# A hybrid decoder step on one core: state pieces loaded one step ahead, their update pinned on ScalarE

## The chip, the cores and the metric

One Trainium2 chip, one NeuronCore (core 0). The metric is the device time of one execution in microseconds; lower is better. The engines are called by the profile's names: PE (TensorE matmuls), PEld (TensorE weight loads), DVE (VectorE), ACT (ScalarE), POOL (GpSimd), SP (SyncE, which issues the weight DMAs here).

## The reference

One inference step of a one-layer decoder for 272 prompt tokens (16 meta tokens and 256 new ones) and 8 sample tokens, each of a running sequence:

```python
u = rmsnorm(h, pre_mix_g)
mix, conv_buf, ssm_h, ret_s = mixers(u, ...)   # SSD heads and retention heads
h = h + rmsnorm(mix @ w_out, post_mix_g)
f = rmsnorm(h, pre_ffn_g)
f = (silu(f @ w_gate) * (f @ w_up)) @ w_down
h = h + rmsnorm(f, post_ffn_g)
```

For the sample tokens the mixers also return the new states, and these concern us here. Each is an old state times a decay plus an outer product with the new token: `hg = exp(last) * hg + (wts * x) B^T` for the 16 SSD heads, `s = exp(c * lg) * s + k v^T` for the 4 retention heads. The SSD states of the 8 sequences are 4 MB, the retention states 8 MB; each has to be read and written back once for the update. They feed nothing else in the step.

## The kernel before

All weights (some 210 MB in fp32) stream through the core in pieces of 128 x 1024, 512 KB each. `Stream.block` (L113) brings one piece in eight blocks: SP loads it into `raw` (4 buffers, L122), ACT copies it into `hi` in a rounded matmul format (3 buffers, L123), and DVE takes the rest `raw - hi` into `lo` (3 buffers, L124). `three` (L130) multiplies each 128 x 128 block with the activations, which are split the same way, in three matmuls: `hi` with the high part (L132), `hi` with the low part (L133), `lo` with the high part (L134). A piece thus serves 24 matmuls, and `gemm` (L136) sums up 16 blocks (2 pieces) in PSUM before its result is evicted.

The stages run in order: the input projection with the mixers between its matmuls, `w_out` (tiles `o`), the two feed-forward matrices (tiles `f`, gate and up blocks in turn, 88 results), and `w_down` (tiles `d`). The change lies in the feed-forward stage. There `ev_f` (L842) evicts each result: for an even one DVE scales it (L846) and ACT takes its silu (L848); for an odd one DVE scales it, multiplies the two (L851), ACT rounds the product into `ah` (L852) and DVE takes the rest into `al` (L853). Up to `m` = 39 of the 44 pairs, 24 of these odd evictions carry a state step. Such a step first copies one column on POOL (`pace`, L857), which waits for L851 and so ties the step to that moment; then it calls `ret_state` (L816, 16 pieces, tile `su`) or `ssm_state` (L825, 8 pieces, tile `hu`), two of the first to one of the second.

One state piece is 128 x 1024, 512 KB: POOL loads it (L819, L828), ACT multiplies it by its decay in place (L820, L829), DVE adds the outer product in 4 instructions of 256 columns (L822) or 8 of 128 columns (L831), and POOL stores it (L86). The pieces live in the pool `sd` with 3 buffers under one tag.

The order on each engine is made when the kernel is built, by a planner that simulates the program and issues what is ready, by priority, which is the place in the program. The `hi` and `lo` of a weight piece are raised by 1500 places. `keep_in_program_order` fixes an instruction behind the last one that was traced on the same engine before it; `pinned` (L219) does so for a POOL DMA. Here `pace` and the load are fixed in this way, while the ACT copy of a state piece stands wherever the planner saw its data ready. At run time each engine takes its instructions strictly in that order.

Of the kernel before, what the change touches and what calls it, by code (L numbers as in the profile page):

```python
# [9 lines left out]
AF = mybir.ActivationFunctionType  # L10
# [5 lines left out]
P = 128  # L16
# [37 lines left out]
def hybrid_step(ctx: ExitStack, tc: tile.TileContext, wall, xT, pp, cc, dmask, cs, convst, ssm, ret,  # L54
                yT, oconv, opssm, opret, osssm, osret):
    nc = tc.nc
    V, A, G, T = nc.vector, nc.scalar, nc.gpsimd, nc.tensor
    MULT, ADD, SUB, MAX, MIN = ALU.mult, ALU.add, ALU.subtract, ALU.max, ALU.min
# [12 lines left out]
    def slot(name, w=NA, n=4, dt=F32):  # L71
        return sp.tile([P, n, w], dt, name=name, tag="s")

    def small(name, w=NA):
        t = ta.tile([P, 308], F32, name=name, tag="t")
        return t[:, :w]

    def bank(name, w=512):
        t = pm.tile([P, 512], F32, name=name, tag="m")
        return t[:, :w]  # L80

    def table(name):
        return tc.keep_in_program_order(A.preload_act_table_set(name))

    def load(out, in_):
        G.dma_start(out, in_)  # L86
# [9 lines left out]
    def con(n, i=0, w=None):  # L96
        w = CC[n][1] - i if w is None else w
        return ccs[:, CC[n][0] + i:CC[n][0] + i + w]
# [55 lines left out]
                three(ps[:, :n], xh, xl, k == 0, k == nk - 1)  # L154
            evict(m, ps[:, :n])

    # u = x * g, split in two parts
    table("sqrt_and_others")
    xs = [slot(f"x{i}") for i in range(4)]
    uh = [slot(f"uh{i}", dt=F32R) for i in range(4)]  # L160
# [29 lines left out]
        i, j = divmod(k, 4)  # L190
        return uh[i][:, j, NA - n:NA], ul[i][:, j, NA - n:NA]

    # token norms
    sxn = cp.tile([P, 64], F32, name="sxn")
    sbn = cp.tile([P, P], F32, name="sbn")
    skn = cp.tile([P, 64], F32, name="skn")
    svn = cp.tile([P, 256], F32, name="svn")
# [8 lines left out]
    def token_norms():  # L206
        pr = bank("pr", NA)
        for i in range(2):
            T.matmul(pr, ones, xsum[:, i, :], start=(i == 0), stop=(i == 1))
        with tc.high_priority(offset=1500):  # L210
            A.activation(rbc, pr, AF.Sqrt, bias=eps, scale=1.0 / DM)
            V.reciprocal(rbc, rbc)

        # rotary tables with the token norm
        for i in range(2):
            V.tensor_tensor(tabs[:, i, :], css[:, i, :], rbc, MULT)
            A.mul(tabs[:, 2 + i, :], tabs[:, i, :], 1.0 / 16.0)

    def pinned(out, in_):  # L219
        tc.keep_in_program_order(G.dma_start(out, in_))  # L220
# [7 lines left out]
            pinned(cst, convst)  # L228
            pinned(dms, dmask)

# [1 line left out]
    bc = slot("bc")  # L232
    xc = [slot(f"xc{i}") for i in range(2)]
    cst = tp.tile([P, 12, NB, 3], F32, name="cst")
# [2 lines left out]
    dasel = cp.tile([P, 1], F32, name="dasel")  # L237
# [90 lines left out]
    def ev_first(m, ps):  # L328
        if m == 0:
            token_norms()  # L330
            held["dt"] = do_dt(ps)
            next(held["dt"])
        else:
            do_xbc(m - 1, ps)
# [6 lines left out]
            next(held["dt"])  # L341
    load(oconv, cout.rearrange("p a b c -> p a (b c)"))

# [1 line left out]
    def nat_lhs(name, src):  # L345
        m = tp.tile([P, NB, 8, 2], F32, name=name, tag="nl", bufs=2)
        for half in range(2):
            for i in range(2):
                V.tensor_scalar(m[:, :, 4 * i:4 * i + 4, half].rearrange("p b t -> p t b"), src[i], con("pm", half, 1),
                                None, MULT)  # L350
        return m.rearrange("p b t h -> p (b t h)")
# [6 lines left out]
    COLS = ((0, 256, 0), (256, 400, 112), (400, 416, 240))  # L358
    MCOLS = ((0, 256, 16), (256, 400, 0), (400, 416, 104))

# [1 line left out]
    y1 = [slot(f"y1_{i}", NO) for i in range(2)]  # L362
    y2 = [slot(f"y2_{i}", NO) for i in range(2)]
    btok = slot("btok", 256, 3)
# [117 lines left out]
                                   ps[:, hp * 8:hp * 8 + 8], MULT, ADD)  # L482
        yield

# [1 line left out]
    kf = [slot(f"kf{i}") for i in range(2)]  # L486
    qf = [slot(f"qf{i}", NO) for i in range(2)]
    vsm = [tp.tile([P, 4, NB], F32, name=f"vsm{i}", tag=f"vsm{i}", bufs=1) for i in range(2)]
# [139 lines left out]
                A.copy(o, ps)  # L628
                load(opret[:, m, :], o)

# [1 line left out]
    def rstds(name, groups, scale, outs=None, load_table=True):  # L632
        pss = []
        for g, sums in enumerate(groups):
            ps = bank(f"{name}{g}", NO)
            for i, s in enumerate(sums):
                T.matmul(ps, ones, s, start=(i == 0), stop=(i == len(sums) - 1))
            pss.append(ps)
        if load_table:
            table("natural_log_exp_and_others")  # L640
        rs = outs or [small(f"{name}r{g}", NO) for g in range(len(groups))]
        sc = scale if isinstance(scale, list) else [scale] * len(groups)
        with tc.high_priority(offset=1000):
            for ps, r, c in zip(pss, rs, sc):
                A.activation(r, ps, AF.Ln, bias=eps, scale=c)
            for r in rs:
                A.activation(r, r, AF.Exp, scale=-0.5)
        return rs
# [97 lines left out]
    for g in (ssd, kt, ssmp, scr, rsm, rsm2, yr, rsq, nrm, n10):  # L746
        assert next(g, None) is None

# [1 line left out]
    def min_(k, n):  # L750
        i, j = divmod(k, 4)
        return mh[i][:, j, :], ml[i][:, j, :]
# [29 lines left out]
    for k in range(KT):  # L782
# [12 lines left out]
        elif k < KT - 1:  # L795
            n = small(f"hs{k}", NO)
# [9 lines left out]
    def ffn_norm():  # L806
        rstds("n4", [[ha, hb]], 1.0 / DM, [rhc], False)

# [1 line left out]
    mix.close()  # L810
    ex = ctx.enter_context(tc.tile_pool(name="ex", bufs=NEXTRA))
    def fin(k, n):
        i, j = divmod(k, 4)
        return fh[i][:, j, :], fl[i][:, j, :]

    def ret_state(c):  # L816
        sb = sd.tile([P, 4, 256], F32, name=f"su{c}", tag="st")
        tc.keep_in_program_order(
            G.dma_start(sb, ret[:, c * 1024:(c + 1) * 1024].rearrange("p (a v) -> p a v", v=256)))  # L819
        A.activation(sb, sb, AF.Copy, scale=con("gam"))  # L820
        for a in range(4):
            V.scalar_tensor_tensor(sb[:, a, :], svn, skn[:, 4 * c + a:4 * c + a + 1], sb[:, a, :], MULT, ADD)  # L822
        load(osret[:, c * 1024:(c + 1) * 1024].rearrange("p (a v) -> p a v", v=256), sb)

    def ssm_state(c):  # L825
        sb = sd.tile([P, 8, P], F32, name=f"hu{c}", tag="st")
        tc.keep_in_program_order(
            G.dma_start(sb, ssm[:, c * 1024:(c + 1) * 1024].rearrange("p (a n) -> p a n", n=P)))  # L828
        A.activation(sb, sb, AF.Copy, scale=dasel)  # L829
        for a in range(8):  # L830
            V.scalar_tensor_tensor(sb[:, a, :], sbn, sxn[:, 8 * c + a:8 * c + a + 1], sb[:, a, :], MULT, ADD)  # L831
        load(osssm[:, c * 1024:(c + 1) * 1024].rearrange("p (a n) -> p a n", n=P), sb)

    def aslot(name, i):
        if i < FT // 4 - NEXTRA // 2:
# [6 lines left out]
    def ev_f(m2, ps):  # L842
        m, up = divmod(m2, 2)
        i, j = divmod(m, 4)
        t = small(f"f{m2}", NO)
        V.tensor_tensor(t, ps, rhc, MULT)  # L846
        if not up:
            A.activation(t, t, AF.Silu)  # L848
            held[m] = t
            return  # L850
        V.tensor_tensor(t, t, held.pop(m), MULT)  # L851
        A.copy(ah[i][:, j, :], t)  # L852
        V.tensor_tensor(al[i][:, j, :], t, ah[i][:, j, :].bitcast(F32), SUB)  # L853
        n = m * 24 // 40
        if m < 40 and (m + 1) * 24 // 40 > n:
            pace = ta.tile([P, 1], F32, name=f"pace{m}", tag="pace", bufs=2)
            tc.keep_in_program_order(G.tensor_copy(pace, t[:, 0:1]))  # L857
            if n % 3 == 2:
                ssm_state(n // 3)
            else:  # L860
                ret_state(n // 3 * 2 + n % 3)

    gemm("f", fin, KT, NO, 0, OUTF, ev_f, outer=OUTF, before=ffn_norm)
    do_pret(PRE, 4)
    do_pssm()
    gemm("f", fin, KT, NO, OUTF, 2 * FT, ev_f)

    def ain(k, n):
# [139 lines left out]
```

## Time and profile before

| | us |
|---|---|
| median of 3 runs | 1303.81 |
| lowest and highest run | 1300.5, 1310.38 |
| span of the profiled execution, first to last instruction | 1292.1 |

The profiled execution is a run of its own; of its time the profile gives only the span. What a run's time holds beyond a span (start and end of the program) is 8.4 us from the lowest run and 11.7 us from the median. All times in the rows are counted in us from the start of the span. A busy PE in them is a modelled one: matmuls overlap, each row shows some 0.28 us, and the next one starts about 0.12 us after it.

### The profile page before, as it was taken

Reading aid. Unit: us, or ns where it says so; the run is one execution under the profiler, and the core shown is the slowest. Engines: PE = TensorE matmul, PEld = TensorE weight load, DVE = VectorE, ACT = ScalarE, POOL = GpSimd, SP = SyncE. Lnnn points to the kernel's source line nnn. Section 1 sums busy time; section 2 is a strip of 40 time slices with the busy share of each in tenths; the row PEclk is TensorE's granted clock in tenths of the full one; section 3 lists DMA queues with packets and bytes.
Section 4 is the critical chain, followed back from the end, with each engine's and each line's share of the span. In section 5 each row is a group of like instructions: output and inputs, shape, how many; then the busy total and the mean of one; then the engine's idle time right before and its main releaser. Section 6 shows DMA issues by size and latency. Waiting matters only on the chain.

```text
span 1292.1 us, 24571 instructions
## 1 busy us (share of the span) xinstructions
PE 1259.5 (97%) x10078; PEld 1242.6 (96%) x10078; DVE 819.6 (63%) x1259; ACT 605.1 (47%) x838; POOL 167.6 (13%) x235
## 2 busy tenths in 40 slices
PE   8999999999999999999999999999999999999994
PEld 8999999999999998899999999999999999999994
DVE  7987879975765469466565566665656544444445
ACT  7665344356854455544444444444444433333331
POOL 3211001110001234210110101011010000000013
PEclk9999999999999999999999999999999999999997
DMA  8665448874565657666766766766666555555562
GB/s 269 207 204 197 146 146 288 274 258 127 157 194 181 180 174 248 197 229 219 250 226 211 249 228 214 244 229 223 234 227 230 181 182 182 183 184 181 181 221 93
DMA packets 74832, 266.41 MB, mean 206 GB/s; under 512 B 8592, under 2 KB 9504, under 8 KB 74720
## 3 DMA queue, kind: packets, MB, share of 16 engines
q1 hardware_dynamic: 60192, 214.17, 50.8%
q0 software_dynamic: 13808, 49.52, 11.3%
q8 instruction: 79, 1.29, 0.4%
q10 hardware_dynamic: 720, 1.16, 0.2%
q14 instruction: 33, 0.27, 0.1%
HBM read 246.15 MB, written 18.66 MB: 205 GB/s over the span
## 4 chain that ended last, share of the span: by engine, by line
PE 39%; DMA 6%; DVE 5%; issue 2%; ACT 1%; DVEq 0%; POOL 0%; POOLq 0%; ACTq 0%
PE d L133 7%; PE d L132 7%; PE d L134 7%; PE f L134 7%; PE f L132 6%; PE f L133 6%; DMA su<-in_dram 3%; DMA hu<-in_dram 3%; DVE lo L124 2%; DVE su L822 1%; ACT su L820 1%; DVE hu L831 1%; ACT hu L829 1%; DVE f L846 1%; DVE p L887 0%
## 5 line engine op out<-in xcount | busy, mean ns | idle before, releaser
L124 DVE TENSOR_TENSOR lo<-raw,hi 128x1024 fp32r<-128x1024 f32 (+1 forms) x405 | 493.1, 1219 | 306.1 <-ACT hi L123 303.1
L123 ACT CAST hi<-raw 128x1024 fp32r<-128x1024 f32 (+1 forms) x405 | 418.7, 1040 | 463.4 <-PE d L133 146.5
L134 PE MATMUL f<-fh,lo 128*128 128x264 f32 x1408 | 400.5, 285 | 9.3 <-DVE lo L124 9.2
L132 PE MATMUL f<-fh,hi 128*128 128x264 f32 x1408 | 400.4, 285 | 1.0 <-ACT fh L654 1.0
L133 PE MATMUL f<-fl,hi 128*128 128x264 f32 x1408 | 400.5, 285 | 0.0
L134 PEld LDWEIGHTS f<-fh,lo 128*128 128x128 f32 x1408 | 265.5, 189 | 12.9 <-DVE lo L124 12.9
L132 PEld LDWEIGHTS f<-fh,hi 128*128 128x128 f32 x1408 | 264.7, 188 | 1.8 <-ACT fh L654 1.4
L133 PEld LDWEIGHTS f<-fl,hi 128*128 128x128 f32 x1408 | 264.7, 188 | 0.5 <-issue 0.2
L133 PE MATMUL d<-al,hi 128*128 128x264 f32 x704 | 200.1, 284 | 0.0
L134 PE MATMUL d<-ah,lo 128*128 128x264 f32 x704 | 200.0, 284 | 0.0
L132 PE MATMUL d<-ah,hi 128*128 128x264 f32 x704 | 199.9, 284 | 0.0
L132 PEld LDWEIGHTS d<-ah,hi 128*128 128x128 f32 x704 | 132.7, 189 | 0.0
L133 PEld LDWEIGHTS d<-al,hi 128*128 128x128 f32 x704 | 132.6, 188 | 0.0
L134 PEld LDWEIGHTS d<-ah,lo 128*128 128x128 f32 x704 | 132.4, 188 | 0.0
L132 PE MATMUL o<-mh,hi 128*128 128x264 f32 x256 | 72.9, 285 | 0.0
L133 PE MATMUL o<-ml,hi 128*128 128x264 f32 x256 | 72.7, 284 | 0.0
L134 PE MATMUL o<-mh,lo 128*128 128x264 f32 x256 | 72.5, 283 | 0.0
L132 PE MATMUL xb<-uh,hi 128*128 128x280 f32 x208 | 62.0, 299 | 2.8 <-ACT hi L123 2.8
L134 PE MATMUL xb<-uh,lo 128*128 128x280 f32 x208 | 60.8, 296 | 1.7 <-DVE lo L124 1.7
L822 DVE SCALAR_TENSOR_TENSOR su<-svn,skn,su 128x256 f32<-128x256 f32 x64 | 26.8, 480 | 55.4 <-ACT su L820 55.4
L133 PE MATMUL xb<-ul,hi 128*128 128x280 f32 x208 | 61.5, 296 | 0.0
L857 POOL COPY pace<-f 128x1 f32<-128x1 f32 x24 | 26.4, 1101 | 210.3 <-DVE f L851 210.3
(298 smaller groups left out, 2019.8 us busy)
## 6 DMA issues: line engine op xcount, KB each, us to landing
raw<-in_dram SPq DMA_DIRECT2D x401, 512.0 KB, 3.7
rs<-in_dram POOLq DMA_DIRECT2D x16, 512.0 KB, 5.5
su<-in_dram POOLq DMA_DIRECT2D x16, 512.0 KB, 5.1
out_dram<-su POOLq DMA_DIRECT2D x16, 512.0 KB, 3.6
hb<-in_dram POOLq DMA_DIRECT2D x8, 512.0 KB, 6.1
hu<-in_dram POOLq DMA_DIRECT2D x8, 512.0 KB, 5.7
out_dram<-hu POOLq DMA_DIRECT2D x8, 512.0 KB, 5.7
lcb<-lcd POOLq DMA_DIRECT2D x4, 544.0 KB, 7.8
```

The lines of the kernel that those rows point to most:

```text
L123: A.copy(self.hi[:, f:f + w], raw[:, f:f + w])
L124: V.tensor_tensor(self.lo[:, f:f + w], raw[:, f:f + w], self.hi[:, f:f + w].bitcast(F32), SUB)
L132: T.matmul(ps, hi, xhi, start=first, stop=False)
L133: T.matmul(ps, hi, xlo, start=False, stop=False)
L134: T.matmul(ps, lo, xhi, start=False, stop=last)
L820: A.activation(sb, sb, AF.Copy, scale=con("gam"))
L822: V.scalar_tensor_tensor(sb[:, a, :], svn, skn[:, 4 * c + a:4 * c + a + 1], sb[:, a, :], MULT, ADD)
L829: A.activation(sb, sb, AF.Copy, scale=dasel)
L831: V.scalar_tensor_tensor(sb[:, a, :], sbn, sxn[:, 8 * c + a:8 * c + a + 1], sb[:, a, :], MULT, ADD)
L846: V.tensor_tensor(t, ps, rhc, MULT)
L857: tc.keep_in_program_order(G.tensor_copy(pace, t[:, 0:1]))
```

## The change

The two functions are split. The first half loads a piece, the second half, which is returned as a function, scales, adds and stores it. A step loads the next piece and then runs the second half for the piece that the step before loaded, so there are 25 steps (the last loads nothing), spread over `m` up to 40. The ACT copy of the update is now fixed behind the ACT instruction traced ahead of it, which is the rounding into `ah` (L852) of the same eviction. Comment lines that the diff also drops are left out.

```diff
-    def ret_state(c):
+    def ret_load(c):
         sb = sd.tile([P, 4, 256], F32, name=f"su{c}", tag="st")
-        tc.keep_in_program_order(
-            G.dma_start(sb, ret[:, c * 1024:(c + 1) * 1024].rearrange("p (a v) -> p a v", v=256)))
-        A.activation(sb, sb, AF.Copy, scale=con("gam"))
-        for a in range(4):
-            V.scalar_tensor_tensor(sb[:, a, :], svn, skn[:, 4 * c + a:4 * c + a + 1], sb[:, a, :], MULT, ADD)
-        load(osret[:, c * 1024:(c + 1) * 1024].rearrange("p (a v) -> p a v", v=256), sb)
-
-    def ssm_state(c):
+        pinned(sb, ret[:, c * 1024:(c + 1) * 1024].rearrange("p (a v) -> p a v", v=256))
+
+        def update():
+            tc.keep_in_program_order(A.activation(sb, sb, AF.Copy, scale=con("gam")))
+            for a in range(4):
+                V.scalar_tensor_tensor(sb[:, a, :], svn, skn[:, 4 * c + a:4 * c + a + 1], sb[:, a, :], MULT, ADD)
+            load(osret[:, c * 1024:(c + 1) * 1024].rearrange("p (a v) -> p a v", v=256), sb)
+        return update
+
+    def ssm_load(c):
         sb = sd.tile([P, 8, P], F32, name=f"hu{c}", tag="st")
-        tc.keep_in_program_order(
-            G.dma_start(sb, ssm[:, c * 1024:(c + 1) * 1024].rearrange("p (a n) -> p a n", n=P)))
-        A.activation(sb, sb, AF.Copy, scale=dasel)
-        for a in range(8):
-            V.scalar_tensor_tensor(sb[:, a, :], sbn, sxn[:, 8 * c + a:8 * c + a + 1], sb[:, a, :], MULT, ADD)
-        load(osssm[:, c * 1024:(c + 1) * 1024].rearrange("p (a n) -> p a n", n=P), sb)
+        pinned(sb, ssm[:, c * 1024:(c + 1) * 1024].rearrange("p (a n) -> p a n", n=P))
+
+        def update():
+            tc.keep_in_program_order(A.activation(sb, sb, AF.Copy, scale=dasel))
+            for a in range(8):
+                V.scalar_tensor_tensor(sb[:, a, :], sbn, sxn[:, 8 * c + a:8 * c + a + 1], sb[:, a, :], MULT, ADD)
+            load(osssm[:, c * 1024:(c + 1) * 1024].rearrange("p (a n) -> p a n", n=P), sb)
+        return update
+
+    fetched = []
+
+    def state_step(n):
+
+        if n < 24:
+            fetched.append(ssm_load(n // 3) if n % 3 == 2 else ret_load(n // 3 * 2 + n % 3))
+        if len(fetched) > 1 or n >= 24:
+            fetched.pop(0)()
 
     def aslot(name, i):
         if i < FT // 4 - NEXTRA // 2:
@@ -851,14 +864,11 @@
         V.tensor_tensor(t, t, held.pop(m), MULT)
         A.copy(ah[i][:, j, :], t)
         V.tensor_tensor(al[i][:, j, :], t, ah[i][:, j, :].bitcast(F32), SUB)
-        n = m * 24 // 40
-        if m < 40 and (m + 1) * 24 // 40 > n:
+        n = m * 25 // 41
+        if m < 41 and (m + 1) * 25 // 41 > n:
             pace = ta.tile([P, 1], F32, name=f"pace{m}", tag="pace", bufs=2)
             tc.keep_in_program_order(G.tensor_copy(pace, t[:, 0:1]))
-            if n % 3 == 2:
-                ssm_state(n // 3)
-            else:
-                ret_state(n // 3 * 2 + n % 3)
+            state_step(n)
 
```

## Rows read from the trace of the kernel before

**Rows 1.** Page, parts 1 and 2: busy us (share) xinstructions; GB/s by slice.

```profile
PE 1259.5 (97%) x10078; PEld 1242.6 (96%) x10078; DVE 819.6 (63%) x1259; ACT 605.1 (47%) x838; POOL 167.6 (13%) x235
...
GB/s 269 207 204 197 146 146 288 274 258 127 157 194 181 180 174 248 197 229 219 250 226 211 249 228 214 244 229 223 234 227 230 181 182 182 183 184 181 181 221 93
```

**Rows 2.** Windows: us, busy (x) of each engine, granted clock, DMA share, GB/s.

```profile
560.00:600.00 40.00, 40.00 (x332) 40.00 (x331) 25.40 (x39) 19.06 (x23) 2.78 (x4) 1.00 0.70 229
600.00:1000.00 400.00, 393.41 (x3218) 390.69 (x3218) 247.29 (x378) 182.74 (x221) 43.64 (x60) 1.00 0.68 229
1000.00:1040.00 40.00, 40.00 (x332) 40.00 (x331) 20.15 (x24) 17.76 (x20) 0.00 (x0) 1.00 0.56 177
1000.00:1240.00 240.00, 240.00 (x1982) 240.00 (x1981) 109.14 (x104) 93.92 (x101) 16.07 (x17) 1.00 0.58 186
```

**Rows 3.** Waits, 600 to 1000: who waited for whom, us in total, times, longest.

```profile
ACT su L820 <- DMA su<-in_dram: 47.4, 13, 4.3
...
ACT hu L829 <- DMA hu<-in_dram: 35.2, 7, 5.5
...
PEld f L134 <- DVE lo L124: 9.1, 12, 1.3
```

**Rows 4.** ACT timeline, 914 to 924: start, us, operation [idle before <-releaser].

```profile
914.08 1.05 ACT L123 CAST hi<-raw 128x1024 fp32r<-128x1024 f32 x1 [0.51 <-PE f L133]
920.65 1.16 ACT L829 ACTIVATE hu<-hu,dasel 128x1024 f32<-128x1024 f32 x1 [5.52 <-DMA hu<-in_dram]
921.71 1.98 ACT L123 CAST hi<-raw 128x1024 fp32r<-128x1024 f32 x2
```

**Rows 5.** Timeline of DVE at the same step.

```profile
921.84 1.40 DVE L831 SCALAR_TENSOR_TENSOR hu<-sbn,sxn,hu 128x128 f32<-128x128 f32 x5 [5.46 <-ACT hu L829]
923.16 1.22 DVE L124 TENSOR_TENSOR lo<-raw,hi 128x1024 fp32r<-128x1024 f32 x1
```

**Rows 6.** Timeline of PE at the same step.

```profile
923.02 0.28 PE L133 MATMUL f<-fl,hi 128*128 128x264 f32 x1
924.43 0.39 PE L134 MATMUL f<-fh,lo 128*128 128x264 f32 x1 [1.12 <-DVE lo L124]
```

**Rows 7.** Timeline of ACT at the step of 601.

```profile
600.66 1.05 ACT L123 CAST hi<-raw 128x1024 fp32r<-128x1024 f32 x1 [1.85 <-PE f L133]
601.67 0.41 ACT L852 CAST ah<-f 128x264 fp32r<-128x264 f32 x1
603.59 1.05 ACT L123 CAST hi<-raw 128x1024 fp32r<-128x1024 f32 x1 [1.50 <-PE f L133]
608.34 1.15 ACT L820 ACTIVATE su<-su,ccs 128x1024 f32<-128x1024 f32 x1 [3.71 <-DMA su<-in_dram]
```

**Rows 8.** Timeline of ACT at the step of 579.

```profile
580.31 1.05 ACT L123 CAST hi<-raw 128x1024 fp32r<-128x1024 f32 x1 [1.50 <-PE f L133]
584.47 1.15 ACT L820 ACTIVATE su<-su,ccs 128x1024 f32<-128x1024 f32 x1 [3.12 <-DMA su<-in_dram]
```

**Rows 9.** Groups by line, DVE, 600 to 1000: busy, mean ns, idle.

```profile
L124 DVE TENSOR_TENSOR lo<-raw,hi 128x1024 fp32r<-128x1024 f32 x135 | 165.0, 1222 | 55.0 <-ACT hi L123 53.4
...
L822 DVE SCALAR_TENSOR_TENSOR su<-svn,skn,su 128x256 f32<-128x256 f32 x52 | 21.7, 480 | 46.5 <-ACT su L820 46.5
L831 DVE SCALAR_TENSOR_TENSOR hu<-sbn,sxn,hu 128x128 f32<-128x128 f32 x56 | 15.9, 346 | 34.7 <-ACT hu L829 34.7
```

**Rows 10.** Timeline of POOL, 901 to 915.

```profile
901.81 0.54 POOL L819 DMA_DIRECT2D su<-in_dram  x1
910.19 0.53 POOL L86 DMA_DIRECT2D out_dram<-su  x1 [7.85 <-ACT hi L123]
...
914.25 0.53 POOL L828 DMA_DIRECT2D hu<-in_dram  x1
```

**Rows 11.** The tile hu: time from issue to landing of its DMAs.

```profile
DMA to landing us min/median/max: 4.8/5.7/6.4
```

## The prediction

> **What bounds the kernel now.** I read the page first: PE is busy for 1259.5 us of a span of 1292.1, ACT for 605.1 [rows 1]. So PE is the bound, and a change on ACT, DVE or POOL is worth what it gives back of PE's gaps, no more. The state steps all lie in the feed-forward stage, so I next cut that stage into windows [rows 2]. The reader is to look at the counts of matmuls there, not only at the busy time. From 1000 to 1240 us, where no state is touched, PE starts (1982 - 332) / 200 = 8.25 matmuls per us, one every 0.121 us. Matmuls that straddle an edge stand in a window twice over, which this difference takes out. At that rate the 400 us from 600 to 1000 would show 332 + 360 x 8.25 = 3302 matmuls, and they show 3218. The 84 that are missing are 84 x 0.121 = 10.2 us. From 560 to 600 us, with state steps in it too, nothing is missing (332, 40.00 us busy). The granted clock is 1.00 in all of these windows, so no clock is involved.
>
> Then the waits say who made the gaps [rows 3]: PE's weight loads waited for `lo` of L124 12 times, 9.1 us, and ACT waited for the landing of state pieces 47.4 us (13 times) and 35.2 us (7 times). The timeline of one step joins the two. ACT ends a `hi` at 914.08 + 1.05 = 915.13, then stands at the copy of `hu` for 5.52 us, until its load has landed, and copies for 1.16 us; the next two `hi` start only at 921.71 [rows 4]. DVE does five of its eight updates at 921.84 and reaches `lo` at 923.16 [rows 5]; PE, which would have gone on 0.12 us after 923.02, starts at 924.43, 1.29 us late [rows 6]. ACT takes its instructions in order, so a late state piece, which nobody needs soon, holds up the weights behind it.
>
> How much of such a hold is free? At 579 ACT's hold from the end of one `hi` to the end of the state copy is 584.47 + 1.15 - (580.31 + 1.05) = 4.3 us [rows 8], and PE loses nothing [rows 2]. At 914 it is 921.81 - 915.13 = 6.7 us and PE loses 1.3. So some 5.4 us are free: two pieces of `hi` and `lo` made ahead.
>
> **The change, part by part.** The waits for the state load leave ACT. ACT gets the copy of a piece that was loaded one step before. The closest steps are 914.25 - 901.81 = 12.4 us apart [rows 10], and a `hu` lands 4.8 to 6.4 us after its issue [rows 11], so at the copy it has been there for 6 us or more. The 20 waits of 82.6 us in sum go to zero. What the 82.6 us cost PE was 10.2 us, and that is the most that this part can bring.
>
> The copy is fixed behind `ah` (L852). It costs ACT 1.15 us as before, 24 times, and stands where ACT has room: behind `ah` of the step at 601 ACT idled for 1.50 us until PE freed a buffer of `hi` [rows 7]. 1.15 goes into 1.50, so its price is zero; if it were not covered, `hi` would be at most 1.15 us late, which the free 5.4 us take. Behind it on ACT stand the `hi` of the coming pieces, and for these DVE and PE wait.
>
> The additions on DVE keep their number: 4 x 0.480 = 1.9 us for a `su`, 8 x 0.346 = 2.8 us for a `hu` [rows 9]. They now come some 4 us earlier, close to the eviction. In the step at 601 `hi` ended at 603.59 + 1.05 = 604.64 and `lo` could follow; a copy right behind `ah` would end at 601.67 + 0.41 + 1.15 = 603.23 [rows 7], so updates queued whole ahead of `lo` would end at 605.1 or 606.0 and hold it for 0.5 or 1.4 us. Of the 5.4 us of hold that are free, the wait of 1.50 was there without any state work, so some 3.9 us of lateness are free, and 1.4 is within them: zero, with an upper bound at what the `hu` steps lose now.
>
> On POOL the load now goes past the store of the step before. A store came 8.4 us behind the load (901.81 to 910.19) because it waited for the update [rows 10]; now it follows sooner, and the next load is issued where it was, behind `pace`. POOL has no other work there that PE needs. The third buffer is enough: the piece that a load replaces was sent off two steps earlier, over 12.4 us, and a store of `hu` lands within 6.4 too [rows 11]. On SP nothing is moved. A 25th step with no load and steps shifted by one `m` at most cost PE nothing: all of it ends before `w_down` has run far, and that stage has no gap at all [rows 2].
>
> Sum: -10.2 us at best; the unknown residue on DVE is 0 to 9 (if the seven `hu` steps of this window went on losing the 1.29 us of [rows 6]: 7 x 1.29). It is nearest to the zero end by the lateness of 1.4 against 3.9, and I take 0.7. That is -9.5 us: a span of 1282.6. The median lies 11.7 us above the span of before, and 1282.6 + 11.7 is 1294.3; I say 1294, 0.7% less.
>
> The Trainium skill (Perfetto Trace Analysis, Identifying the Most-Contended Engine) says that matmul busy time is a poor measure, since pipelined matmuls mislead, and that the busy share of weight loads is to be read instead. PE's busy time alone would make the loss 400 - 393.41 = 6.6 us, a time of about 1298; the weight loads make it 400 - 390.69 = 9.3 us, 1295 [rows 2]. The trace agrees with the rule: the count of matmuls gives 10.2, on the weight loads' side.
>
> **The rivals.**
>
> *The `hu` steps go on losing.* If the planner queues DVE's eight updates and the eviction ahead of `lo`, and the lead is smaller than I read it, the `hu` steps still lose up to 1.29 us each. For it: the eight small updates are DVE's longest block in a step, and `lo` waits between them [rows 5]. Against: 1.4 us late against 3.9 free. Between half of the 9 us and all of them stay lost, the gain is 10.2 - 4.5 to 10.2 - 9.0, or 1.2 to 5.7 us: 1298 to 1302.6, say 1300.
>
> *Nothing moves.* ACT still waits, because the load itself comes late (its buffer is not free, or the copy stands ahead of its turn). That would need a landing over 12.4 us after `pace`, against 6.4 at most. 1304.
>
> *The DMA engines become the bound; slower.* Today ACT's standing still also pauses the weight stream, so the state load has the engines nearly to itself. Afterwards the stream runs on, and a load and the store of the piece before are under way at once: some 181 GB/s of weights [rows 1] and 1 MB in about 8 us, 131 GB/s, together 312 GB/s, while the highest slice shows 288 [rows 1]. Weights would then lag by 24 GB/s x 8 us = 0.2 MB, 0.7 us. `raw` has four buffers, so more than 5 us of lag are covered, and the lead of `hi` and `lo` lies behind that. It decides only if a weight piece lands over 9 us late; each microsecond beyond costs 24 us in all, so at one microsecond 24 - 10 = +14: 1318. Against it: slices of 288 and 274 GB/s early in the kernel, and a DMA share of 0.68 in this stage.
>
> **How the numbers follow.** Most of the gaps gone: 0.70, with its own range of 1290 to 1298, by the spread of the runs shown. `hu` steps go on: 0.16. Nothing moves: 0.07. DMA bound: 0.07. A difference of 1% is 13 us, about what a measurement of this kernel can tell from no change (three runs lie within 10). The whole loss that can come back is 10.2 us, so "faster by over 1%" needs a lucky draw of the runs: 0.10. Slower by over 1% is the DMA case: 0.06. The rest is 0.84. The range goes from 1288 (the full 10.2 us measured from a run near the lowest, 1300.5, and a little more) to 1303, which takes in the second case and leaves out the third and fourth.
>
> **What would show it.** Right: ACT's waits for `su` and `hu` are gone from the list of waits; the copies stand directly behind `ah`; PE's wait for `lo` in the feed-forward stage is near zero; 400 us of that stage hold some 3290 to 3302 matmuls; the `w_down` stage begins about 9.5 us earlier and is as long as before. Wrong: weight loads that still wait for `lo`, and then behind L831 (the first rival), `hi` that waits for the landing of `raw` for microseconds (the DMA rival), or copies that still wait for a landing. A gain of more than 11 us in the span would mean that I missed a loss outside of PE's gaps.

## The result, and the profile after

The changed kernel takes 1283.45 us (median of 4 runs, 1283.2 to 1285.46), the kernel before 1302.15 (4 runs, 1299.42 to 1310.38): a ratio of 0.9867, with a 95% interval of 0.9837 to 0.9897. That is 18.7 us, or 1.3%, where 1294 us and 0.7% were forecast; the time lies 4.5 us under the range. The profiled execution took 1283.67 us with a span of 1281.8, and here lies the first surprise: only 1.9 us stand around the span, not the 11.7 that the prediction added, and not the 8.4 to 11.7 that the section on the time before puts down to the start and end of the program.

The first line of the chain that ended last, on the page of the kernel before:

```profile
PE 39%; DMA 6%; DVE 5%; issue 2%; ACT 1%; DVEq 0%; POOL 0%; POOLq 0%; ACTq 0%
```

The page of the changed kernel, its span, part 1 and the same line:

```profile
span 1281.8 us, 24583 instructions
...
PE 1255.2 (98%) x10078; PEld 1240.1 (97%) x10078; DVE 825.6 (64%) x1259; ACT 608.0 (47%) x838; POOL 170.0 (13%) x236
...
PE 93%; DVE 3%; DMA 1%; issue 1%; ACT 1%; SPq 0%; POOL 0%; DVEq 0%; ACTq 0%
```

Before, the chain went through the landings of state pieces, through DVE and through ACT (it could be followed back to 603 us only, so its shares add up to 53% of the span); now it is followed back through nearly the whole span, and 93% of that is PE. PE's busy time fell by 4 us only [rows 1], which says little, for the reason that the prediction gave: a busy PE is modelled.

The same windows as [rows 2], for PE alone:

```profile
560.00:600.00 40.00, 40.00 (x333) 1.00 0.69 228
600.00:1000.00 400.00, 400.00 (x3302) 1.00 0.70 235
...
1000.00:1240.00 240.00, 240.00 (x1982) 1.00 0.57 188
```

From 600 to 1000 us there are 3302 matmuls, the number that the prediction worked out for a stage without gaps (3218 before). `w_down` has the rate that it had. The feed-forward stage is 10.1 us shorter, from 531 us to its end, and the stages on both sides are as long as they were.

The waits of that stretch, answering to [rows 3]:

```profile
ACT hi L123 <- PE f L133: 148.4, 83, 1.9
...
POOL out_dram L86 <- DVE su L823: 25.5, 13, 2.0
ACT hi L123 <- ACT su L821: 6.2, 14, 0.4
```

ACT waits for no state load any more, and no wait of PE is left in the list. What ACT waits for now is PE itself: `hi` stands still until PE has freed a buffer, which is how a stage looks that PE bounds. The step that answers to [rows 7], on ACT, then on DVE, then on POOL:

```profile
600.46 1.05 ACT L123 CAST hi<-raw 128x1024 fp32r<-128x1024 f32 x1 [1.85 <-PE f L133]
601.47 0.42 ACT L865 CAST ah<-f 128x264 fp32r<-128x264 f32 x1
601.79 1.15 ACT L821 ACTIVATE su<-su,ccs 128x1024 f32<-128x1024 f32 x1
603.38 1.06 ACT L123 CAST hi<-raw 128x1024 fp32r<-128x1024 f32 x1 [0.44 <-ACT su L821]
```

```profile
602.69 0.43 DVE L866 TENSOR_TENSOR al<-f,ah 128x264 fp32r<-128x264 f32 x1
603.03 1.67 DVE L823 SCALAR_TENSOR_TENSOR su<-svn,skn,su 128x256 f32<-128x256 f32 x4
604.62 1.22 DVE L124 TENSOR_TENSOR lo<-raw,hi 128x1024 fp32r<-128x1024 f32 x1
```

```profile
602.75 0.54 POOL L220 DMA_DIRECT2D su<-in_dram  x1
605.24 0.53 POOL L86 DMA_DIRECT2D out_dram<-su  x1 [1.95 <-ACT hi L123]
...
614.39 0.54 POOL L220 DMA_DIRECT2D hu<-in_dram  x1
```

The copy of the older piece follows `ah` directly, into the 1.50 us in which ACT idled before; 0.44 us of idling are left and `hi` starts as early after `ah` as it did. The four additions stand between `al` and `lo`, and `lo` starts at 604.62, 0.18 us behind the end of its `hi`. POOL loads the next piece at 602.75 and stores the older one at 605.24, 2.5 us later, where 8.4 us lay between load and store [rows 10]; the next load is at 614.39, 11.6 us on. The piece loaded at 602.75 took 8.0 us to land by the trace, longer than any in the five profiles of the kernel before that this text uses (7.0 at most), and no engine waited for it.

### The profile page after: what moved, and what is told of

Its sections match the earlier page's. It is cut to its first block, busy times and chain, and to the rows that moved or that the text cites. A ratio compares the mean times of both kernels' runs of the same rounds, so it can differ in the third digit from the quotient of the medians.

```text
span 1281.8 us, 24583 instructions
## 1 busy us (share of the span) xinstructions
PE 1255.2 (98%) x10078; PEld 1240.1 (97%) x10078; DVE 825.6 (64%) x1259; ACT 608.0 (47%) x838; POOL 170.0 (13%) x236
## 3 DMA queue, kind: packets, MB, share of 16 engines
q8 instruction: 79, 1.29, 0.4%
q10 hardware_dynamic: 720, 1.16, 0.2%
## 4 chain that ended last, share of the span: by engine, by line
PE 93%; DVE 3%; DMA 1%; issue 1%; ACT 1%; SPq 0%; POOL 0%; DVEq 0%; ACTq 0%
PE f L132 13%; PE f L133 13%; PE f L134 13%; PE d L133 7%; PE d L132 7%; PE d L134 7%; PE o L132 2%; PE o L133 2%; PE o L134 2%; PE xb L133 1%; PE xb L134 1%; PE xb L132 1%; PE k L132 1%; PE v L132 1%; PE v L133 1%; PE k L133 1%
## 5 line engine op out<-in xcount | busy, mean ns | idle before, releaser
L870 POOL COPY pace<-f 128x1 f32<-128x1 f32 x25 | 29.2, 1166 | 343.8 <-DVE f L864 343.8
L859 DVE TENSOR_TENSOR f<-f,rhc 128x264 f32<-128x264 f32 x88 | 37.6, 432 | 48.8 <-PE f L134 48.5
```

## The experiments

**Where the other 8 us come from.** The steps of the prediction hold in the two profiles: 10.3 us of span between them, against 9.5 forecast and 10.2 as the most. The question was why the times differ by 18.7. Theory A: the one profiled execution of before had less loss than most. Rival B: something around the span. The kernel before was run again, unchanged:

> The kernel before, unchanged, to see the span of each of its timed executions. Theory A (the state loads' landing time differs from one execution to the next, and each longer landing is paid on PE): each execution's span lies only about 1.9 us under its time, as in the changed kernel (1283.67 and 1281.8), so spans of 1297 to 1308 appear, and a profile of such a span shows waits of ACT for the state pieces well over 82.6 us and more than 84 missing matmuls between 600 and 1000 us. Rival B (start and end of the program cost 10 us in the kernel before and 2 us in the changed one): all spans stay within 2 us of 1292.1 and the times lie 8 to 12 us above them.

Its 12 executions have spans of 1293.7 to 1305.6 us, each 1.7 to 1.9 us under its time, and the 17 executions beside them 1293.4 to 1306.8. Rival B is out. The execution of the prediction, at 1292.1, was shorter than all of these 29. Three more profiles show where a longer one has its time:

> The kernel before, unchanged, profiled once more, to see where an execution of another length has its time. Theory A: the span less 1281.8 us is the matmuls missing between 600 and 1040 us, 10 to 20 us, plus 0 to 4 us of the stall near 90 us; the more ACT waited for the state landings in sum (82.6 us gave 10.2 us, 85.5 gave 14), the more PE lost, at near one for one. Rival H: the feed-forward loss is 10 to 14 us in each, and the rest lies in other stages.

> As the look before it: another execution of the kernel before, with the same expectations.

> As the two looks before it: a third execution of the kernel before, with the same expectations.

The longest of them, the first look: the window, and the waits in it.

```profile
600.00:1000.00 400.00, 386.69 (x3143) 1.00 0.67 223
```

```profile
ACT su L820 <- DMA su<-in_dram: 54.4, 13, 5.4
...
ACT hu L829 <- DMA hu<-in_dram: 36.0, 7, 6.1
```

ACT waited 90.4 us for landings (82.6 in [rows 3]) and 3302 - 3143 = 159 matmuls are missing, 159 x 0.121 = 19.3 us instead of 10.2. All five profiles of the kernel before and two of the changed one, by the same two views, by the matmuls between 80 and 100 us, of which the best execution of the changed kernel shows 149, and by two stretches of the trace: from the start to the first matmul on `f`, and from there to the first on `d`. What follows on that is 274.1 us long in all seven.

| execution | span | ACT's waits, 600 to 1000 | matmuls missing there | matmuls, 80 to 100 | up to the first `f` | first `f` to first `d` |
|---|---|---|---|---|---|---|
| before, of the prediction | 1292.1 | 82.6 | 84 | 142 | 477.3 | 540.7 |
| before, again | 1299.1 | 85.5 | 114 | 109 | 480.7 | 544.4 |
| before, first look | 1304.3 | 90.4 | 159 | 120 | 480.4 | 549.9 |
| before, second look | 1299.7 | 82.5 | 93 | 110 | 482.7 | 543.0 |
| before, third look | 1299.8 | 84.4 | 110 | 120 | 481.3 | 544.5 |
| changed | 1281.8 | 0 | 0 | 149 | 477.1 | 530.6 |
| changed, again | 1284.8 | 0 | 0 | 126 | 480.2 | 530.6 |

So both theories of these looks are partly right. By the count the feed-forward stage loses 10.2 to 19.3 us between 600 and 1000 us, 13.6 on average (112 matmuls), and not 10.2; by its whole length it loses 10.1 to 19.3, 13.9 on average, since two of the looks lose a little before 600 us too. The rest of the spread, some 3 to 5 us, lies ahead of that stage, for the most part in a second stall near 90 us, which has nothing to do with the state steps (their first load comes behind 520 us) and which the changed kernel has too. Of the 8.6 us by which the four later executions of the kernel before are longer than the first, 4.7 on average lie in the feed-forward stage and 3.9 ahead of it. On the same sum of waits the second look loses more than the first profile, so the sum is not what decides.

What decides is each hold by itself. I took, for the 101 steps behind 590 us in the five profiles, ACT's hold as the prediction did (end of a `hi` to end of the state copy) and PE's gaps around it. A hold under 4.8 us cost nothing, in all cases. Above that, a `su` cost its hold less 4.8 us, a `hu` its hold less 5.0, within 0.1 us, with one exception. (No `hu` was held for less than 5.6 us, so its 5.0 is worked out from the losses of longer holds.) The exception is the step of the first look at 681:

```profile
680.75 1.05 ACT L123 CAST hi<-raw 128x1024 fp32r<-128x1024 f32 x1 [0.17 <-PE f L133]
687.94 1.16 ACT L829 ACTIVATE hu<-hu,dasel 128x1024 f32<-128x1024 f32 x1 [6.13 <-DMA hu<-in_dram]
```

The hold is 687.94 + 1.16 - (680.75 + 1.05) = 7.3 us and PE lost 3.7 us, 1.4 more than the rule. The windows of PE just behind it say why:

```profile
688.00:692.00 4.00, 2.31 (x17) 1.00 0.00 1
...
692.00:696.00 4.00, 4.00 (x24) 0.62 0.81 232
```

PE was busy for 2.31 us of 4.00, and in the next 4 us the granted clock is 0.62 on the mean, so it fell from the full 2.4 GHz to the 1.2 GHz level for a part of them: 24 matmuls, where 4 us at full speed show some 34.

**The early load without the pin.** Is the pin needed? And is it enough alone? The second needs no run: with the pin but without the early load, every engine has the same instructions in the same order as in the kernel before. The first:

```diff
-            tc.keep_in_program_order(A.activation(sb, sb, AF.Copy, scale=con("gam")))
+            A.activation(sb, sb, AF.Copy, scale=con("gam"))
...
-            tc.keep_in_program_order(A.activation(sb, sb, AF.Copy, scale=dasel))
+            A.activation(sb, sb, AF.Copy, scale=dasel)
```

> The change without the pin on ACT: pieces are loaded one step ahead, the ACT copy is left to the planner. Theory A with the order the planner makes (it puts the copy one weight piece behind its own load, where it stood in the kernel before): ACT waits for the landings as before, some 80 us or more in all, PE loses 10 us or more, ratio 0.99 to 1.01 against the kernel before. Rival C (loading early is the part that does it, the pin is an ornament): ACT's waits are gone and the ratio is that of the full change, 0.985 to 0.989.

It takes 1320.71 us, a ratio of 1.0147 (1.0121 to 1.0174): slower than the kernel before, and outside of the range that theory A gave. Its stretch from 600 to 1000 us, one step on POOL and on ACT, and the waits:

```profile
600.00:1000.00 400.00, 382.59 (x3038) 0.97 0.64 218
```

```profile
617.02 0.54 POOL L86 DMA_DIRECT2D out_dram<-su  x1 [9.49 <-issue]
...
619.54 0.54 POOL L220 DMA_DIRECT2D hu<-in_dram  x1
632.29 0.53 POOL L86 DMA_DIRECT2D out_dram<-hu  x1 [12.21 <-DVE hu L834]
```

```profile
618.45 0.41 ACT L865 CAST ah<-f 128x264 fp32r<-128x264 f32 x1 [1.06 <-DVE f L864]
619.26 1.05 ACT L123 CAST hi<-raw 128x1024 fp32r<-128x1024 f32 x1 [0.39 <-PE f L133]
626.88 1.15 ACT L832 ACTIVATE hu<-hu,dasel 128x1024 f32<-128x1024 f32 x1 [6.57 <-DMA hu<-in_dram]
```

```profile
ACT su L821 <- DMA su<-in_dram: 57.8, 13, 7.1
...
ACT hu L832 <- DMA hu<-in_dram: 29.8, 6, 7.0
```

The copy at 626.88 is that of the piece whose load was issued at 619.54, in the same step. Nothing but its load holds the second half of a step, so the planner, in whose simulation the load must have landed by then, pulls it forward to one `hi` behind its own `ah`: the place it had in the kernel before. The early load is undone, and the hold is 626.88 + 1.15 - (619.26 + 1.05) = 7.7 us. Six of the 20 holds are over 7 us here, worked out in the same way. The trace shows what goes with these late landings. Eight of the 24 loads were issued while the store of the piece before them, issued 2.5 to 3.3 us earlier, was still under way, as at 617.02 and 619.54; they landed in 6.8 to 7.7 us. The other 16 landed in 4.3 to 7.0 us, 15 of them within 5.9. In the five profiles of the kernel before, no state load was issued while a state store was under way. That the store is the cause is not shown by a run of its own. PE's clock pays on top, here behind the step near 680:

```profile
688.00:691.00 3.00, 1.47 (x10) 1.00 0.01 3
691.00:695.00 4.00, 3.25 (x16) 0.57 0.49 145
```

PE stood for half of the three microseconds, and the next four have 0.57 of the clock. From 600 to 1000 us 3302 - 3038 = 264 matmuls are missing, 32 us; by the rule of the holds it would be 22, and the clock lacks 0.03 x 400 = 12.

**A later landing, with and without the change.** To raise the one suspected cost, half of each piece is loaded a second time, which has to wait for the first load:

```diff
+        pinned(sb[:, 0:2, :], ret[:, c * 1024:c * 1024 + 512].rearrange("p (a v) -> p a v", v=256))
...
+        pinned(sb[:, 0:4, :], ssm[:, c * 1024:c * 1024 + 512].rearrange("p (a n) -> p a n", n=P))
```

> The kernel before, with the first half of each state piece loaded a second time behind the whole of it into the same place, so the piece is complete some 3 to 5 us later (the second load waits for the first to land, then 256 KB land). Theory A: every hold of ACT grows by this, all are then above the free 5.4 us, and PE loses 24 x 3 to 5 us more, 70 to 120 us: 1370 to 1420 us. Rival D (what PE loses comes from the DMA traffic or from DVE's updates, not from the landing): a few us more than before, 1303 to 1312.

> The changed kernel with the same second load of the first half. Theory A: the piece is complete 9 to 11 us after its step began, the closest steps are 11.6 us apart, so ACT waits for nothing or nearly nothing and the time stays within 3 us of the changed kernel, 1283 to 1287. Rival D (the traffic itself is what costs): as many us more as the kernel before gains by the same second load.

The kernel before goes to 1353.99 us, 1.0392 (1.0354 to 1.043). That is 53 us more and not the 70 to 120 expected. The same stretch, and a step of it on POOL and on ACT:

```profile
600.00:1000.00 400.00, 368.30 (x2874) 0.97 0.64 217
```

```profile
690.90 0.53 POOL L829 DMA_DIRECT2D hu<-in_dram  x1
696.15 0.54 POOL L220 DMA_DIRECT2D hu<-in_dram  x1 [4.72 <-DMA hu<-in_dram]
```

```profile
689.82 0.41 ACT L854 CAST ah<-f 128x264 fp32r<-128x264 f32 x1 [1.81 <-DVE f L853]
690.13 1.05 ACT L123 CAST hi<-raw 128x1024 fp32r<-128x1024 f32 x1
691.92 1.05 ACT L123 CAST hi<-raw 128x1024 fp32r<-128x1024 f32 x1 [0.73 <-ACT hi L123]
...
699.18 1.15 ACT L831 ACTIVATE hu<-hu,dasel 128x1024 f32<-128x1024 f32 x1 [5.90 <-DMA hu<-in_dram]
```

The copy comes 8.3 us after the first load's issue in this step (6.4 in [rows 4] and [rows 10]); over the 24 steps of the trace it comes after 9.7 us on the mean, against 5.3 to 5.7 in the five profiles of the kernel before, so the landing is some 4 us later, as expected. But the planner, which knows of the second load, lets two `hi` pass before the copy instead of one, in all steps but the first, and the hold is counted from the last of them: it is 7.3 us on the mean, against 5.3 in the execution of the prediction. By the rule above the holds from 600 to 1000 us cost 41 us; 3302 - 2874 = 428 matmuls are missing, which is 52 us. The difference is about what the clock lacks at a mean of 0.97: 0.03 x 400 = 12 us. The sign and the cause are as expected; the size was taken too large, because a later landing was taken for an equally longer hold. The changed kernel with the same second load:

```profile
600.00:1000.00 400.00, 400.00 (x3301) 1.00 0.75 248
```

No matmul is missing (3301 against 3302), and the time is 1286.98 us, ratio 0.988 (0.9853 to 0.9907). The 3.5 us above the first runs of the changed kernel are the stall near 90 us: PE's one wait there was 3.3 us in this profile and 0.8 in that of the changed kernel, and the first matmul on `f` comes 3.5 us later (480.6 against 477.1). So 6 MB more through the same queue and later landings cost the changed kernel nothing in this stage.

**Half the lead.** The update runs at the next even eviction, two weight pieces after its load, fixed there behind the silu:

```diff
             A.activation(t, t, AF.Silu)
             held[m] = t
+            if fetched:
+                fetched.pop(0)()
             return
...
-        if len(fetched) > 1 or n >= 24:
-            fetched.pop(0)()
...
-        n = m * 25 // 41
-        if m < 41 and (m + 1) * 25 // 41 > n:
+        n = m * 24 // 40
+        if m < 40 and (m + 1) * 24 // 40 > n:
```

> The update is not run at the next step but at the next even eviction, two weight pieces (5.8 us) after its load's step, and fixed there behind the silu; 24 steps as in the kernel before. Theory A (a hold of ACT below some 5 us is free): the load, issued 1.3 us after the step begins and 5 to 8 us in landing, is up to 3 us late, ACT waits 0 to 3 us each time, 20 to 50 us between 600 and 1000 us, the holds stay under 5 us, and PE loses nothing: 1283 to 1286, as the changed kernel. Rival F (any wait of ACT for a landing is paid on PE in part): 1288 to 1296.

1286.24 us, ratio 0.9877 (0.9846 to 0.9909). ACT's waits for landings between 600 and 1000 us, and one step:

```profile
ACT hu L832 <- DMA hu<-in_dram: 2.2, 2, 1.5
ACT su L821 <- DMA su<-in_dram: 1.9, 3, 0.8
```

```profile
610.93 0.41 ACT L859 ACTIVATE f<-f 128x264 f32<-128x264 f32 x1
611.32 1.15 ACT L821 ACTIVATE su<-su,ccs 128x1024 f32<-128x1024 f32 x1
612.89 1.05 ACT L123 CAST hi<-raw 128x1024 fp32r<-128x1024 f32 x1 [0.42 <-PE f L133]
```

ACT waits 4.1 us in all, less than the 20 to 50 expected, since most landings come in time; PE's feed-forward stage has no gap (3301 matmuls from 600 to 1000 us). Its spans, 1282.8 to 1285.9, are those of the changed kernel with the early stall. A whole step of lead is thus more than is needed: 5.8 us do, as long as the copy has a fixed place.

**What is left of the state steps.** Without them (the column copies on POOL stay):

```diff
-            state_step(n)
```

> The changed kernel without the state steps: the new states of the sample tokens are neither loaded, updated nor stored (24 pieces, 12 MB in and 12 MB out, 24 ACT copies and 128 DVE updates are left out), to price what is left of them. Theory A: they cost PE nothing in the changed kernel, so this is within 1 us of it in span, 1281 to 1282 (3.4 us more where the stall near 90 us falls long). The residue of 0.7 us that the prediction took would show as 1281. Rival G (traffic and updates still cost several us): 1275 to 1279.

```profile
600.00:1000.00 400.00, 400.00 (x3301) 1.00 0.57 181
```

The profiled span is 1281.7 us, against 1281.8 with the steps, and from the first matmul on `f` to the first on `d` it is 530.6 us in both. DMA traffic falls from 235 to 181 GB/s, and PE does not notice. The residue of 0.7 us that the prediction took is not there. (The median of its four runs, 1286.51, is higher, with spans of 1281.7 to 1287.2. The early stall may be the reason; only the shortest of the four was profiled, so this is not shown.)

**The changed kernel again, and the stall near 90 us.**

> The changed kernel, unchanged, beside the kernel before on one chip, to see the span of each execution. Theory A (with the state landings off the path, what made the kernel before differ from execution to execution is gone): spans within 4 us of each other, 1281.5 to 1285.5, the upper ones with the 3.4 us that a stall near 90 us costs (it has nothing to do with the state steps); the kernel before spreads over 10 us or more. Rival E (the spread is the chip's, and any kernel has it): a spread of 10 us here too.

1284.68 us against 1301.29 for the kernel before on that chip, ratio 0.9863 (0.983 to 0.9897); spans of 1281.8 to 1284.8, while the kernel before spreads from 1292.3 to 1306.4. The spread of 14 us was the kernel's, not the chip's. What remains is the early stall, and it is the same illness: DVE's differences of the step decays (L305) wait in order for a broadcast load, with `lo` behind them. A last kernel runs them later and fixes their place, beside the changed kernel:

```diff
-        if 7 <= m < 10:
+        if m in (7, 8, 12):
             next(held["dt"])
...
-            V.tensor_tensor(wj[:, :, 4 * i:4 * i + 4],
+            tc.keep_in_program_order(V.tensor_tensor(wj[:, :, 4 * i:4 * i + 4],
...
+                    if h < 2:
+                        tc.keep_in_program_order(ins)
```

> The changed kernel with the same cure where the same illness shows near 85 to 92 us: DVE's differences of the step decays (L305, and the first L404 behind them) wait in DVE's order up to 4.6 us for the landing of the broadcast loads of lcb, and `lo` behind them makes PE wait 0.8 to 3.3 us. Here L305 runs after the last result of that stage and it and the first six L404 are fixed in DVE's program order. Theory A: the wait for lcb is gone, PE's wait for `lo` in 70 to 110 us is under 1 us, the spans lie within 2 us of each other at 1279 to 1282, ratio 0.982 to 0.986. Rival I (the work that moves late takes DVE's time where the next stage needs it, or shows a new wait): the same as the changed kernel or slower, 1284 to 1292.

> The changed kernel, unchanged, on the same chip, to compare with the late lcb: spans 1281.5 to 1285.5 as before, the upper ones with 2 to 4 us of the stall near 90 us.

The changed kernel's waits and windows in that stage, then the windows of the late one:

```profile
DVE wj L305 <- DMA lcb<-lcd: 5.3, 3, 3.9
...
PE xb L134 <- DVE lo L124: 2.2, 1, 2.2
```

```profile
80.00:90.00 10.00, 8.92 (x69) 1.00 0.82 306
90.00:100.00 10.00, 8.93 (x57) 0.83 0.55 172
```

```profile
80.00:90.00 10.00, 10.00 (x80) 1.00 0.90 280
90.00:100.00 10.00, 10.00 (x79) 1.00 0.83 291
```

DVE's wait and PE's are gone and 80 + 79 matmuls stand where 69 + 57 stood. It takes 1282.57 us (1282.18 to 1284.02), the changed kernel beside it 1284.58 (1282.74 to 1286.17); against the kernel before on that chip 0.9873 (0.9852 to 0.9895) and 0.9887 (0.9869 to 0.9905). The spans are 1280.4 to 1282.2, within the 2 us of each other that were expected; the ratio lies above the 0.982 to 0.986 expected. In the late kernel's profile the first matmul on `f` comes at 477.5 us, against 479.7 in the changed kernel beside it, but 477.1 in the best profile of that kernel: what is cured is the long form of the stall. The 2 us between the medians lie within ranges that overlap, so that it is faster than the changed kernel is likely and not settled.

## Why the prediction was right, and where it was wrong

*What bounds the kernel, and the count of 10.2 us*: right for the execution that it was read from. That execution lost 84 matmuls in the stretch, the changed kernel loses none, and the spans differ by 10.3 us. The reading by matmul counts was right where PE's busy time (6.6 us) was not.

*The waits leave ACT; the price of the copy is zero; DVE's updates hold `lo` within its lead; POOL's order is harmless*: right, each in the rows after. `lo` came 0.18 us behind its `hi`, against the 0.5 that the prediction allowed a `su`. The third buffer is enough.

*The free part of a hold, "some 5.4 us"*: a little high. It is 4.8 us for a `su` and 5.0 for a `hu`; at the step of 914 PE lost 1.6 us, in the wait of 1.29 and three gaps of 0.1 around it that were not counted.

*The residue of 0.7 us*: too high; the kernel without state steps shows none.

*"The median lies 11.7 us above the span of before, and 1282.6 + 11.7 is 1294.3"*: this is the step that failed. The distance between a median of other executions and the span of the profiled one was taken for time around the span, which every kernel has. What stands around a span is 1.7 to 1.9 us in every execution with both on record. Of the 10.8 us between 1294.3 and 1283.45, 9.9 are this term, 11.7 instead of 1.8; the span itself was forecast within about 1 us (1282.6; the four are 1281.4 to 1283.7). In place of the term the runs showed losses inside the spans of longer executions, of two kinds. One is the loss that the profile showed and the change cures: the term "10.2 us at best" was mis-sized for the typical execution, 13.9 us on average of five profiles and up to 19.3. The other lies ahead of that stage, for the most part in the early stall; it made the four later executions of the kernel before some 4 us longer, and the change does not cure it.

The three runs of before were in sight, 1300.5 to 1310.38 against a span of 1292.1, and asked for this reading: a spread of 10 us in the kernel before, when PE's rate is constant, is itself a loss.

A part of the 18.7 us is likely luck. On the first chip the early stall was short in the runs of the changed kernel (spans 1281.4 to 1283.7); on the two others the change is worth 16.6 and 14.6 us by the medians, nearer to the 13.9 of the stage that it touches. How the 1302.15 of before divides on the first chip stays open, since the spans of those runs are not on record.

*The rivals*: none came. The `hu` steps lose nothing. "Nothing moves", for the reason that the copy stands ahead of its turn, is what the early load without its pin does, and it is worse than nothing: the prediction gave the pin no term of its own, though the early load hangs on it. The DMA engines did not become the bound, not with the second load either. One premise of that rival was misread: while ACT stands, the state load does not have the engines nearly to itself. From 616 to 621 us, in the first hold of a `hu` in the window, the kernel before kept them 0.99 busy at 356 GB/s, more than the 312 that the rival added up.

## What to carry to other kernels

An in-order engine that feeds the bound engine should reach work on a load only when that load has surely landed; loading early does this only if the consumer's place in the order is fixed as well, since a planner that believes the load lands sooner pulls the consumer forward again. The lead of the buffers decides what a late landing costs: here holds below 4.8 us were free and each microsecond above was paid in full, so a sum or a mean of waits says little. Set the span of the one profile against the spread of the times before taking what lies between for overhead: where the times spread, price the profile's losses for the typical execution.

## What the runs showed of the hardware that was not expected

The landings of the same 512 KB pieces differ between executions of one program on one chip. The feed-forward stage is 6.9 us longer in the first look than in the second (549.9 and 543.0 us); the longest landing wait of ACT in the stretch was 6.1 us in the one and 5.5 in the other. With a state store under way at its issue, a load took 6.8 to 7.7 us to land (the early load without the pin). The Trainium skill (DMA: Bandwidth & Descriptors, Latency and other measured facts) has the latency of the main memory vary with its load; the spread here fits that in kind, while no run shows which part of a landing varies.

PE's clock fell to the 1.2 GHz level after a stall that left PE busy for 1.47 of 3 us, with matmuls in between, and the lower clock then stretched the next microseconds: granted clocks of 0.57 and 0.62 in the stretches shown. A stall of PE can so cost more than its gap. The Trainium skill (TensorE: Matmul & The Clock Gate, What's actually happening) says that the clock is set by how busy the engine has been recently; the traces agree.
